# A decoder step on one core: three deferred tiles for four, their loads ahead of the stores of x, and two tags for the PSUM of the down projection

## The chip, the cores and the metric

The kernel runs on one core of a Trainium2 chip. The metric is the device time of one execution in microseconds (us). TensorE does the matrix products, VectorE and ScalarE the elementwise work, GpSimd part of it; all DMAs are issued by SyncE's queue (SPq in the profile). All data are float32; the weight products are made of three products of high and low parts.

## The reference

One inference step of a decoder layer, for a prompt of 1024 tokens and 8 x 8 sample tokens (1088 columns in all, model width 1024):

```python
h = rms_norm(x, norm_mix_g)
proj = h @ w_in
a = silu(layer_norm(depthwise_conv_valid(a_full, ...)))       # convolution heads
o = attend(q, k, v)                                            # dilated attention
x = x + concat([a, o]) @ w_out
h = rms_norm(x, norm_ffn_g)
g_full = concat([ffn_past, h @ w_ffn_gate])
g = depthwise_conv_valid(g_full, ffn_conv_w, ffn_conv_b)
x = x + (silu(g) * (h @ w_ffn_up)) @ w_ffn_down
y = rms_norm(x, norm_final_g)
```

The K and V rows and the last rows of both convolutions are outputs too.

## The kernel before

Everything is held transposed: features on the 128 partitions, tokens along the free dimension. `x` is 8 tiles of 128 features. Weights come in tiles of 128 output features. Every operand of a weight product is split into a high part (ScalarE, a rounding copy) and a low part (a subtraction on VectorE or GpSimd), and `block_product` (L916) and `two_products` (L931) issue three matmuls for each pair of tiles and each chunk of 272 tokens.

The order on each engine and queue is made by a planner from a simulated timeline; the code steers it with `tc.issue_after(i)`, which puts the instructions of a block behind instruction `i` on its engine, and with the number of buffers of each tag. Memory comes in zones; a tile of a new zone waits for the tiles of the old zone whose place it takes.

The stages that matter here:

- **Output projection.** The 8 feature tiles of the mixed heads (`mixed`, spilled to DRAM) go into `w_out` in `PARTS` (3, 3, 2). `out_part` (L855) does a part for all 8 output tiles m, all tokens. In the second part the tiles m in `ORDER[:DEFER]` do only the first half of the tokens (544 columns, `HALF`); the second half of these is deferred.
- **The last part** is done by halves of the tokens: `out_half(0)` and `out_half(1)` (L1099). For each m a pair of PSUM banks (`pair`, L906) takes the product of the last two features, VectorE adds it to x (L1111), x is stored to DRAM (`x2d`, L1112), ScalarE squares it (L1114) and VectorE sums the squares (L1118). In `out_half(1)` the deferred tiles add their three missing features (`deferred`, `wd`). The deferred operands are loaded with L1013 and converted between the tiles of `out_half(0)` (`convert`: `later_input`, L998, `later_weight`, L1004).
- **Second norm.** `root` (L201) sums the squares over the partitions with tiny matmuls and takes the inverse root; `spread` (L226) copies it to all partitions. The first half's root is made inside `out_half(1)` (`norm_first`), the second half's between the first two products of the gate (`between`, `spread_second`).
- **Gated feed-forward, zone F.** The tokens' halves and the weights' halves are combined in seven block products, with their block tiles in the tags b11, b21, b22, t1 to t4 of 8 buffers each. The first pair of weight tiles is done with plain products: `gate0` and `up0` with `first_half` and `second_half`. After it `ffn_pair` for j = 1 to 10 runs the seven products (`products`, L1212), whose PSUM pairs px, py, pz turn in four buffers.
- **Down projection, zone D.** Nine units (14 products) over two groups of features; in each unit four chains m = 0 to 3, each in a PSUM pair, are added to x (L1515). Its first five moving tiles (`ux`) are split by L1409 and L1410, and the last four writers of u in zone F (`late[-4:]`) are put behind the fifth of them on VectorE. `last_product` follows with the last features and the final norm; its PSUM banks come from a pool that is opened where the pairs were.

Of the kernel before, what the change touches and what calls it, by code (L numbers as in the profile page):

```python
# [18 lines left out]
F32 = mybir.dt.float32  # L19
# [5 lines left out]
P = 128  # L25
D = 1024
# [36 lines left out]
ORDER, DEFER = (4, 5, 6, 7, 0, 1, 2, 3), 4  # L63
# [19 lines left out]
def trunk_kernel(tc, xT, w_in, w_out, w_gate, w_up, w_down, par, kc, vc, sa, sf, pmask, smask,  # L83
                 yT, kT, vT, ca, cas, cf):
    nc = tc.nc
    with (
# [112 lines left out]
        rooted, summed = [None], [None]  # L199
# [26 lines left out]
        def spread(r, new, width):  # L226

            size = sizes(width)
            rb = new("rb")
            for c0 in range(0, width, 512):  # L230
                pb = bank(*rbank[0])
                w = min(512, width - c0)
                for i in range(c0 // P, -(-(c0 + w) // P)):
                    n = size[i]
                    summed[0] = nc.tensor.transpose(pb[:, i * P - c0:i * P - c0 + n],
                                                    r[:n, i:i + 1].to_broadcast([n, P]), ident[:n, :n]).ins
                nc.scalar.activation(rb[:, c0:c0 + w], pb[:, :w], AF.Copy)
            return rb
# [667 lines left out]
        def pair(s="g"):  # L906

            return zone[pairs[0] + "ps"].tile([P, 1024], F32, tag="g2", name=nm(s), bufs=pairs[1])
# [59 lines left out]
        n = PARTS[-1]  # L968
        part = []
        for h, tag in enumerate(("b11", "t2")):  # L970
            part.append([])
            for i in range(n):
                raw = slot("b11", "mx", F32)
                last_load = nc.sync.dma_start(raw, mixed[k0 + i][:, h * HN:h * HN + HN]).ins
                hi, lo = early[tag].pop() if early[tag] else slot(tag, "mh"), slot(tag, "ml")
                nc.scalar.activation(hi, raw, AF.Copy)
                nc.vector.tensor_sub(lo, raw, hi.bitcast(F32))
                part[h].append((hi, lo))
# [15 lines left out]
        n1 = PARTS[-2]  # L994
        kd = k0 - n1
        deferred, wd, later = [], {}, []

        def later_input(raw):  # L998
            hi, lo = slot("t3", "mh"), slot("t3", "ml")
            nc.scalar.activation(hi, raw, AF.Copy)  # L1000
            nc.gpsimd.tensor_sub(lo, raw, hi.bitcast(F32))
            deferred.append((hi, lo))

        def later_weight(m, raw):  # L1004
            hi, lo = [slot("b22", t, w=n1 * P) for t in ("wh", "wl")]
            nc.scalar.activation(hi, raw, AF.Copy)
            nc.gpsimd.tensor_sub(lo, raw, hi.bitcast(F32))
            wd[m] = [t.rearrange("p (k c) -> p k c", c=P) for t in (hi, lo)]

        def load_later(dst, src):  # L1010
            nonlocal last_load
            with tc.issue_after(last_load):
                last_load = nc.sync.dma_start(dst, src).ins  # L1013

        for i in range(n1):
            raw = slot("t2", "mx", F32)
            load_later(raw, mixed[kd + i][:, HN:])
            later.append((later_input, raw))
        for m0 in ORDER[:DEFER:2]:
            raw = wp.tile([P, D], F32, tag="WR", name=nm("wr"), bufs=WR)[:, :2 * n1 * P]  # L1020
            load_later(raw.rearrange("p (m c) -> p m c", m=2),
                       w_out[m0:m0 + 2, :, kd * P:k0 * P].rearrange("m p c -> p m c"))
            for i in range(2):
                later.append((later_weight, m0 + i, raw[:, i * n1 * P:(i + 1) * n1 * P]))

        def convert(j, square):
            for call, *args in later[j - 1:j] if j else ():
                with tc.issue_after(square):
                    call(*args)

        blocks = {tag: [None] * 4 for tag in BTAGS}
        made = []

        def split(x, tag, k):
            hi, lo = slot(tag, tag + "h"), slot(tag, tag + "l")
            nc.scalar.activation(hi, x, AF.Copy)
            made.append(nc.vector.tensor_sub(lo, x, hi.bitcast(F32)).ins)
            blocks[tag][k] = hi, lo
# [14 lines left out]
        def weight_parts(x, new, eng):  # L1053
            n = x.shape[-1]
            hi, lo = new
            nc.scalar.activation(hi, x, AF.Copy)
            eng.tensor_sub(lo, x, hi.bitcast(F32))
            hi, lo = [t.rearrange("p (k c) -> p k c", c=P) for t in (hi, lo)]
            return [(hi[:, i:i + 4], lo[:, i:i + 4]) for i in range(0, n // P, 4)]

        def block_tile(x, zone=False, eng=nc.gpsimd):

            if zone:
                t = early["gate"].pop(0) if early["gate"] else zt("F", "WA", 2, "wa", D, F32R)
# [3 lines left out]
            nc.scalar.activation(hi, x, AF.Copy)  # L1068
            eng.tensor_sub(lo, x, hi.bitcast(F32))  # L1069
            return [t.rearrange("p (k c) -> p k c", c=P) for t in (hi, lo)]  # L1070

        def plain_blocks(raw):
            return [block_tile(r[:, i * half:i * half + half], r is raw[0]) for r in raw for i in range(2)]
# [22 lines left out]

        x2d = [dp.tile([P, N], F32, name=f"x2d{m}") for m in range(KT)]

        def out_half(h, hook):  # L1099
# [4 lines left out]
            for j, m in enumerate(ORDER):  # L1104
# [7 lines left out]
                nc.sync.dma_start(x2d[m][:, c], x)  # L1112
                s = slot("t1", "sq", F32)
                square = nc.scalar.activation(s, x, AF.Square).ins  # L1114
# [4 lines left out]
                hook(j, square)  # L1119
# [9 lines left out]
        sq0, _ = out_half(0, convert)  # L1129
        rs = []  # L1130

        def norm_first(j, square):
# [12 lines left out]
        raw, up0 = weight_raw(w_up, 0), []  # L1145
# [25 lines left out]
        def between():  # L1171
            rs.append(root(sq1, D, HN))
            with tc.issue_after(rooted[0]):
                for i in range(2):
# [9 lines left out]
        first_blocks(0, "b11")  # L1184
        first_blocks(4, "b21")
# [171 lines left out]
        pairs[:] = ["D", 4]  # L1357
# [129 lines left out]
        for k, (g, unit) in enumerate(UNITS):  # L1487
# [203 lines left out]
```

## Time and profile before

| | us |
|---|---|
| median of 3 runs | 1345.58 (1344.97 to 1346.34) |
| the profiled execution | 1341.79 |
| its span, first to last instruction | 1340.1 |
| TensorE busy | 1294.4 (97%) |
| VectorE busy | 936.2 (70%) |
| ScalarE busy | 561.6 (42%) |
| GpSimd busy | 486.6 (36%) |

In the profile PE is TensorE, PEld its weight loads, DVE VectorE, ACT ScalarE, POOL GpSimd and SPq SyncE's queue of DMAs. A row names the line of the kernel, the operation and its tiles (out<-in, buffer numbers left out). Times in the views count from the start of the span. Neighbouring matmuls overlap: each lasts some 0.29 us, and a new one starts every 0.125 us.

### The profile page before, as it was taken

To read this page: it belongs to the slowest core of one execution; us is meant where nothing else is said; L and a number is where in the kernel's file an instruction comes from. 1 tells how busy PE (TensorE), PEld (TensorE's weight loads), DVE (VectorE), ACT (ScalarE), POOL (GpSimd) and SP (SyncE) were. 2 spreads that over 40 slices of the span, in tenths; PEclk is the share of its full clock that TensorE was granted. 3 is DMA by queue.
4 is the path that set the end of the run, shared out by engine and by line. 5 is a ranking of instruction groups with operands and counts; after the bars stand their busy time and mean duration, and the time that the engine had idled before them with its cause. 6 is when DMAs were issued, how large, how long until landed. Compare 5 with 4: busy or idle time off the path is not lost.

```text
span 1340.1 us, 25967 instructions
## 1 busy us (share of the span) xinstructions
PE 1294.4 (97%) x10311; PEld 1251.1 (93%) x10311; DVE 936.2 (70%) x1785; ACT 561.6 (42%) x1130; POOL 486.6 (36%) x394
## 2 busy tenths in 40 slices
PE   8999999999989998999999999999999989999996
PEld 7999988998979787999999999999999989999996
DVE  6379879555675666578976767667776549967656
ACT  6412121547575466355443323333333434334432
POOL 1321112111101103640765646555465525445610
PEclk9999999999999999999999999999999999999998
DMA  8248777565789868561033322233222394352412
GB/s 312 58 137 298 277 240 199 174 173 137 219 252 258 259 221 256 166 211 61 11 112 122 110 103 72 83 122 106 106 71 84 123 360 164 107 186 86 156 40 95
DMA packets 93738, 211.90 MB, mean 158 GB/s; under 512 B 13873, under 2 KB 43313, under 8 KB 93617
## 3 DMA queue, kind: packets, MB, share of 16 engines
q1 hardware_dynamic: 93616, 210.24, 48.1%
q8 instruction: 81, 1.33, 0.4%
q14 instruction: 41, 0.33, 0.1%
HBM read 154.17 MB, written 56.04 MB: 157 GB/s over the span
## 4 chain that ended last, share of the span: by engine, by line
PE 81%; DVE 9%; DMA 5%; ACT 2%; issue 1%; POOL 1%; SPq 1%; DVEq 0%; POOLq 0%; ACTq 0%
PE g L186 6%; PE g L187 6%; PE g L188 6%; PE py L928 5%; PE py L927 5%; PE py L925 4%; PE g L925 4%; PE g L928 4%; PE g L927 4%; PE px L925 3%; PE pz L925 3%; PE pz L927 3%; PE pz L928 3%; PE px L928 3%; PE px L927 3%; PE s L657 3%
## 5 line engine op out<-in xcount | busy, mean ns | idle before, releaser
L162 POOL TENSOR_TENSOR wl<-wr,wh 128x1024 fp32r<-128x1024 f32 (+1 forms) x36 | 67.9, 1887 | 271.7 <-PE g L188 166.2
L186 PE MATMUL g<-xh,wh 128*128 128x384 f32 (+1 forms) x472 | 156.9, 332 | 1.5 <-DVE qkv L449 1.4
L187 PE MATMUL g<-xl,wh 128*128 128x384 f32 (+1 forms) x472 | 155.2, 329 | 0.0
L188 PE MATMUL g<-xh,wl 128*128 128x384 f32 (+1 forms) x472 | 155.2, 329 | 0.0
L925 PE MATMUL g<-ux,as 128*128 128x272 f32 x504 | 145.8, 289 | 3.8 <-DVE u L1314 3.4
L928 PE MATMUL g<-ux,as 128*128 128x272 f32 x504 | 146.0, 290 | 0.0
L927 PE MATMUL g<-ux,as 128*128 128x272 f32 x504 | 145.4, 289 | 0.0
L1069 POOL TENSOR_TENSOR wb<-wr,wb 128x512 fp32r<-128x512 f32 x82 | 120.1, 1475 | 55.4 <-ACT wb L1068 55.4
L1425 POOL TENSOR_TENSOR as<-ar,as 128x640 fp32r<-128x640 f32 (+1 forms) x56 | 91.1, 1638 | 107.6 <-ACT as L1424 105.7
L1068 ACT ACTIVATE wb<-wr 128x512 fp32r<-128x512 f32 x84 | 52.5, 627 | 155.7 <-DVE wr L1085 95.1
L1069 POOL TENSOR_TENSOR wa<-wr,wa 128x512 fp32r<-128x512 f32 x42 | 65.4, 1560 | 126.6 <-ACT wa L1068 124.6
L925 PEld LDWEIGHTS g<-ux,as 128*128 128x128 f32 x504 | 95.7, 190 | 4.4 <-issue 4.4
L928 PEld LDWEIGHTS g<-ux,as 128*128 128x128 f32 x504 | 95.5, 190 | 0.0
L927 PEld LDWEIGHTS g<-ux,as 128*128 128x128 f32 x504 | 95.4, 189 | 0.0
L186 PEld LDWEIGHTS g<-xh,wh 128*128 128x128 f32 x472 | 88.7, 188 | 3.9 <-DVE qkv L449 2.2
L1295 DVE SCALAR_TENSOR_TENSOR fc<-gb,prm,fc 128x1104 f32<-128x1104 f32 x44 | 81.5, 1870 | 14.8 <-ACT fc L1293 14.4
L698 ACT ACTIVATE y<-y,m 128x128 f32<-128x128 f32 (+1 forms) x192 | 88.5, 465 | 4.9 <-DVE m L686 4.7
L187 PEld LDWEIGHTS g<-xl,wh 128*128 128x128 f32 x472 | 88.8, 188 | 0.1
L188 PEld LDWEIGHTS g<-xh,wl 128*128 128x128 f32 x472 | 88.8, 188 | 0.1
L160 ACT ACTIVATE wh<-wr 128x1024 fp32r<-128x1024 f32 (+1 forms) x36 | 29.5, 821 | 131.1 <-PE g L188 111.0
L399 DVE SCALAR_TENSOR_TENSOR cacc<-gp,prm,cacc 128x1024 f32<-128x1024 f32 x60 | 84.3, 1405 | 0.1
L661 DVE CUSTOM_DVE_ANT_0 y<-s,pmk 128x128 f32<-128x128 f32 (+1 forms) x192 | 63.6, 377 | 28.9 <-PE s L657 24.2
(379 smaller groups left out, 4297.6 us busy)
## 6 DMA issues: line engine op xcount, KB each, us to landing
cr<-in_kc SPq DMA_DIRECT2D x24, 768.0 KB, 8.0
cr<-in_vc SPq DMA_DIRECT2D x24, 768.0 KB, 7.2
ux<-ub SPq DMA_DIRECT2D x63, 272.0 KB, 4.1
kk<-dk SPq DMA_DIRECT2D x48, 256.0 KB, 5.9
wr<-in_w_gate SPq DMA_DIRECT2D x22, 512.0 KB, 3.3
wr<-in_w_up SPq DMA_DIRECT2D x22, 512.0 KB, 4.4
wr<-in_w_in SPq DMA_DIRECT2D x20, 512.0 KB, 4.7
ub<-u SPq DMA_DIRECT2D x18, 544.0 KB, 4.6
```

What stands on the lines that cost most here:

```text
L162: lo_eng.tensor_sub(lo, raw, hi.bitcast(F32))
L186: nc.tensor.matmul(ps[c], whi[:, k, :], xh[:, t0:t0 + n], start=(k == 0), stop=False)
L187: nc.tensor.matmul(ps[c], whi[:, k, :], xl[:, t0:t0 + n], start=False, stop=False)
L188: nc.tensor.matmul(ps[c], wlo[:, k, :], xh[:, t0:t0 + n], start=False, stop=(k == nk - 1))
L399: eng.scalar_tensor_tensor(acc[:, :S], gp[:, j:j + S], col(w0 + j), acc[:, :S], op0=ALU.mult, op1=ALU.add)
L698: nc.scalar.activation(y, y, AF.Exp, bias=m[:, 4 * g + i:4 * g + i + 1], scale=-1.0, accum_out=den[:, g, 2 * hd + u, i:i + 1])
L925: nc.tensor.matmul(ps, whi[:, k, :], xh[:, t], start=(start and k == 0), stop=False, skip_group_check=True)
L927: nc.tensor.matmul(ps, whi[:, k, :], xl[:, t], start=False, stop=False, skip_group_check=True)
L928: nc.tensor.matmul(ps, wlo[:, k, :], xh[:, t], start=False, stop=(stop and k == nk - 1), skip_group_check=True)
L1069: eng.tensor_sub(lo, x, hi.bitcast(F32))
L1295: nc.vector.scalar_tensor_tensor(c[:, :W], gb[i][:, t:t + W], col(C_FW + 3 * f + t), c[:, :W], op0=ALU.mult, op1=ALU.add)
L1425: nc.gpsimd.tensor_sub(lo, raw, hi.bitcast(F32))
```

## The change

- `DEFER` goes from 4 to 3: tile m=7 does all its tokens in the second part.
- The deferred features are loaded straight into the buffers of their low parts (tag t3), the deferred weights into buffers of their own (tag b22), all right behind the loads of the last part; the conversions follow its high parts on ScalarE and go on without the tiles of `out_half(0)` (`parts_of`).
- The stores of x are put behind these loads on the queue.
- The raw tiles of `w_up`'s first pair get four buffers of tag t2 (halves), no longer the two shared ones of `WR`; those and the `w_gate` tiles are loaded behind the last deferred load.
- The four conversions of `gate0` are put behind the copy of the first root on ScalarE, the four of `up0` behind the fourth `b11` part. The low parts of `up0` are made by GpSimd and not by VectorE.
- The first root is made after the first tile of `out_half(1)` and spread after the second (before: second and third); the first scalings follow the second residual, not the third.
- In zone D the four PSUM pairs of one tag become two tags of two: m = 0, 1 use g3, m = 2, 3 use g2. One unused pair of g2 is taken first, so that g2's place comes first.

```diff
-ORDER, DEFER = (4, 5, 6, 7, 0, 1, 2, 3), 4
+ORDER, DEFER = (4, 5, 6, 7, 0, 1, 2, 3), 3
...
-                nc.scalar.activation(rb[:, c0:c0 + w], pb[:, :w], AF.Copy)
+                copied[0] = nc.scalar.activation(rb[:, c0:c0 + w], pb[:, :w], AF.Copy).ins
...
+        def parts_of(raw, hi, lo):
+            done = nc.scalar.activation(hi, raw, AF.Copy).ins
+            nc.gpsimd.tensor_sub(lo, raw, hi.bitcast(F32))
+            return done
...
+        for i in range(n1):
             hi, lo = slot("t3", "mh"), slot("t3", "ml")
+            raw = lo.bitcast(F32)
+            with tc.issue_after(last_load):
+                last_load = nc.sync.dma_start(raw, mixed[kd + i][:, HN:]).ins
+            with tc.issue_after(last_high):
+                last_high = parts_of(raw, hi, lo)
             deferred.append((hi, lo))
+        for m in ORDER[:DEFER]:
+            raw = slot("b22", "wr", F32, n1 * P)
+            with tc.issue_after(last_load):
+                last_load = nc.sync.dma_start(raw, w_out[m, :, kd * P:k0 * P]).ins
             hi, lo = [slot("b22", t, w=n1 * P) for t in ("wh", "wl")]
+            with tc.issue_after(last_high):
+                last_high = parts_of(raw, hi, lo)
...
-        for i in range(n1):
-            raw = slot("t2", "mx", F32)
-            load_later(raw, mixed[kd + i][:, HN:])
-            later.append((later_input, raw))
-        for m0 in ORDER[:DEFER:2]:
-            raw = wp.tile([P, D], F32, tag="WR", name=nm("wr"), bufs=WR)[:, :2 * n1 * P]
-            load_later(raw.rearrange("p (m c) -> p m c", m=2), ...)
...
+        raw = [r for t in weight_raw(w_gate, 0) for r in split_halves(t)]
+        gate_parts, gate0 = plain_blocks(raw, [*map(split_halves, early["gate"]), new_blocks(), new_blocks()])
+        raw = [slot("t2", "wr", F32, half) for _ in range(4)]
+        for i, r in enumerate(raw):
+            with tc.issue_after(last_load):
+                nc.sync.dma_start(r, w_up[i // 2 * HF][:, i % 2 * half:i % 2 * half + half])
+        tiles = [[t[:, :half] for t in early["up"][i:i + 2]] for i in (0, 2)]
+        up_parts, up0 = plain_blocks(raw, [*tiles, new_blocks(), new_blocks()])
...
-                nc.sync.dma_start(x2d[m][:, c], x)
+                with tc.issue_after(last_load):
+                    nc.sync.dma_start(x2d[m][:, c], x)
...
-        sq0, _ = out_half(0, convert)
+        sq0, _ = out_half(0, lambda j: None)
...
-            if j == 1:
+            if j == 0:
                 rs.append(root(sq0, D, HN))
-            elif j == 2:
+            elif j == 1:
                 rs[0] = spread(rs[0], new_root, HN)
+                order = copied[0]
+                for x in gate_parts:
+                    with tc.issue_after(order):
+                        order = parts_of(*x)
...
-                with tc.issue_after(made[-2] if len(made) > 1 else residuals[2]):
+                with tc.issue_after(made[-2] if len(made) > 1 else residuals[1]):
...
-        gate0 = plain_blocks(weight_raw(w_gate, 0))
-        raw, up0 = weight_raw(w_up, 0), []
...
         def between():
             rs.append(root(sq1, D, HN))
-            with tc.issue_after(rooted[0]):
-                for i in range(2):
-                    up0.extend(weight_parts(raw[0][:, i * half:i * half + half], early["up"][2 * i:2 * i + 2],
-                                            nc.vector))
-                up0.extend(block_tile(raw[1][:, i * half:i * half + half], eng=nc.vector) for i in range(2))
...
         first_blocks(0, "b11")
+        order = high[0]
+        for x in up_parts:
+            with tc.issue_after(order):
+                order = parts_of(*x)
         first_blocks(4, "b21")
...
-        pairs[:] = ["D", 4]
+        pairs[:] = ["D", 2]
+        pair()
...
-                        chain[m] = pair()
+                        chain[m] = pair("g", "g3" if m < 2 else "g2")
```

More of the change, by code (lines that the diff above doesn't have):

```diff
@@ L1026, in convert @@
[L1026 to L1029, printed above, removed]
         blocks = {tag: [None] * 4 for tag in BTAGS}
[L1032 removed]
+        made, high = [], [None]
         def split(x, tag, k):
             hi, lo = slot(tag, tag + "h"), slot(tag, tag + "l")
[L1036 removed]
+            high[0] = nc.scalar.activation(hi, x, AF.Copy).ins
             made.append(nc.vector.tensor_sub(lo, x, hi.bitcast(F32)).ins)
@@ L1051, in weight_raw, with block_tile @@
             return raw
[L1053 to L1061, printed above, removed]
+        def block_tile(x, zone=False):
             if zone:
-                t = early["gate"].pop(0) if early["gate"] else zt("F", "WA", 2, "wa", D, F32R)
+                t = zt("F", "WA", 2, "wa", D, F32R)
             else:
```

45 lines of the change are left out of this document (18 added, 27 removed).

## The prediction

> **What bounds the kernel now.** I read the page's busy times first, then the busy time by stretches of 5 us (columns: length, busy time and instruction count of TensorE, its weight loads, VectorE, ScalarE and GpSimd, then the granted TensorE clock).
>
> ```profile
> PE 1294.4 (97%) x10311; PEld 1251.1 (93%) x10311; DVE 936.2 (70%) x1785; ACT 561.6 (42%) x1130; POOL 486.6 (36%) x394
> ```
>
> TensorE is busy 97% of the span, so a change can gain only where TensorE waits, or where it runs at a lower clock. Three such places lie in code that the change touches.
>
> ```profile
> 560.00:565.00 5.00, 2.81 (x14) 2.37 (x14) 3.00 (x3) 3.75 (x6) 4.41 (x4) 0.80 0.71 254
> 565.00:570.00 5.00, 5.00 (x37) 5.00 (x36) 2.52 (x4) 0.69 (x2) 0.00 (x0) 0.86 0.16 59
> 570.00:575.00 5.00, 5.00 (x42) 5.00 (x41) 4.85 (x8) 4.14 (x7) 2.37 (x2) 1.00 0.88 205
> 575.00:580.00 5.00, 2.84 (x18) 2.18 (x18) 4.63 (x6) 3.25 (x7) 5.00 (x4) 1.00 1.04 394
> 580.00:585.00 5.00, 5.00 (x30) 5.00 (x29) 1.54 (x2) 0.16 (x1) 3.47 (x3) 0.66 0.75 242
> ...
> 600.00:605.00 5.00, 5.00 (x42) 5.00 (x41) 5.00 (x8) 2.64 (x4) 0.00 (x0) 1.00 0.39 142
> ...
> 615.00:620.00 5.00, 3.54 (x31) 3.26 (x30) 2.14 (x9) 2.04 (x5) 0.00 (x0) 1.00 0.00 0
> ```
>
> ```profile
> 1075.00:1080.00 5.00, 5.00 (x42) 5.00 (x42) 2.67 (x6) 1.97 (x3) 0.22 (x1) 1.00 0.93 325
> 1080.00:1085.00 5.00, 1.60 (x14) 1.42 (x13) 4.97 (x8) 0.00 (x0) 0.00 (x0) 1.00 1.02 358
> 1085.00:1090.00 5.00, 5.00 (x30) 5.00 (x29) 1.50 (x4) 1.95 (x3) 0.00 (x0) 0.66 1.03 404
> ```
>
> An undisturbed stretch holds 42 matmuls of 272 columns. So 560 to 570 misses 33 of 84, which is 33 / 42 x 5 = 3.9 us (a); 575 to 585 misses 36, 4.3 us (b); 615 to 620 misses 11, 1.3 us (c); 1080 to 1090 misses 40, 4.8 us (d). The list of waits from 560 to 1082 (us in total, times, longest) says for whom TensorE waited, and its own timeline where (start, length, and in brackets the idle time before).
>
> ```profile
> PE py L928 <- POOL wb L1069: 1.8, 1, 1.8
> PE g L925 <- ACT mh L976: 1.7, 1, 1.7
> PE g L235 <- DVE rr L223: 1.5, 1, 1.5
> PE g L925 <- ACT wh L1006: 1.3, 2, 0.9
> PE g L928 <- POOL wl L1007: 0.9, 1, 0.9
> ```
>
> ```profile
> 560.08 0.28 PE L188 MATMUL g<-mh,wl 128*128 128x272 f32 x1
> 562.07 0.77 PE L925 MATMUL g<-mh,wh 128*128 128x272 f32 x4 [1.71 <-ACT mh L976]
> ...
> 1084.41 0.36 PE L925 MATMUL g<-ux,as 128*128 128x272 f32 x1 [3.40 <-DVE u L1314]
> ```
>
> (a) is the start of the last output part (L976), (b) the deferred weights (L1006, L1007), (c) the second root (L223), (d) the first down projection, which waits for an eviction. After 1.7, 2.2 and 3.4 us of waiting a slow stretch follows (clock 0.80 and 0.86, 0.66, 0.66); after 1.5 us in (c) the clock stays 1.00. [...]
>
> **The change part by part.** *Three tiles deferred.* For m=7 the second half (3 features x 3 products x 2 chunks, 18 matmuls) moves from the last output half to the part before it: 18 / 42 x 5 = 2.1 us. No work is saved, but TensorE now ends that part at 560.36 + 2.1 = 562.5, after ScalarE's first high part let it go on at 562.07. Loads and conversions that (a) waited for do not depend on m=7's extra products. Left in (a): the first pair of PSUM banks may wait for m=7's last eviction, 0.72 us by the eviction rows below. Bounds 0 and the whole 3.9; I take 0.7, because 1.5 us in (c) cost no clock. Gain 3.2.
>
> *Loads ahead of the stores.* The DMA queue's timeline:
>
> ```profile
> 558.53 1.33 SPq L974 DMA_DIRECT2D mx<-mixed  x3
> 568.23 0.32 SPq L1112 DMA_DIRECT2D x2d<-x  x1
> 568.65 1.67 SPq L1013 DMA_DIRECT2D mx<-mixed  x3
> 570.42 0.90 SPq L1013 DMA_DIRECT2D wr<-in_w_out  x2
> ```
>
> and GpSimd's:
>
> ```profile
> 572.63 5.54 POOL L1001 TENSOR_TENSOR ml<-mx,mh 128x544 fp32r<-128x544 f32 x3 [8.22 <-ACT mh L1000]
> 578.13 5.34 POOL L1007 TENSOR_TENSOR wl<-wr,wh 128x384 fp32r<-128x384 f32 x4
> 587.08 2.52 POOL L1069 TENSOR_TENSOR wa<-wr,wa 128x512 fp32r<-128x512 f32 x2 [3.61 <-ACT wa L1068]
> 589.57 3.00 POOL L1069 TENSOR_TENSOR wb<-wr,wb 128x512 fp32r<-128x512 f32 x2
> 638.03 9.58 POOL L1069 TENSOR_TENSOR wa<-wr,wa 128x512 fp32r<-128x512 f32 x1 [45.46 <-ACT wa L1068]
> ```
>
> The deferred loads left at 568.65 to 571.3, behind the first store. Now they follow the loads that end at 559.9, so some 8.8 us earlier; the conversions that began at 572.63 can begin near 564 to 566. Three feature lows and one weight low take 5.54 + 5.34 / 4 = 6.9 us, done near 572.5. TensorE needs them after the first half's 96 matmuls (11.4 us) at 562.5 + 0.7 + 11.4 = 574.6. So (b) goes, 4.3; at worst 1.5 of it stays (no landing time was kept). The queue gets three issues more (three weight tiles for two pairs, four halves of `w_up` for two tiles), 1.33 / 3 = 0.44 us each; with the twelve loads it is through by about 565.2, before the first store of x has anything to store at 568.23: nothing lost, and if it were, the scaling that rewrites x would wait for the store.
>
> *Weights bound later, root a tile earlier.* The four `w_gate` conversions follow the copy of the first root, the four of `w_up` follow the fourth `b11` high part and go from VectorE to GpSimd. The gate's 2.52 + 3.00 = 5.5 us of GpSimd have a tile of 30 matmuls and five of 12 to hide behind, 90 matmuls or 10.7 us; beyond that the first gate product would wait. The root's products move from the second tile to the first, 30 matmuls or 3.6 us. VectorE is full behind it (5.00 of 5.00 at 600). What GpSimd costs it:
>
> ```profile
> 577.86 3.78 DVE L1118 TENSOR_TENSOR sq<-sq,sq 128x544 f32<-128x544 f32 x3 [0.26 <-ACT sq L1114]
> ...
> 645.73 0.72 DVE L1206 TENSOR_TENSOR x<-x 128x544 f32<-128x544 f32 x1
> 646.37 0.65 DVE L1278 TENSOR_TENSOR gb<-pv,ta 128x480 f32<-128x480 f32 x1
> ...
> 1079.23 3.26 DVE L1410 TENSOR_TENSOR ux<-ux 128x544 fp32r<-128x544 f32 x5 [0.21 <-DMA x<-x2d]
> 1082.41 1.22 DVE L1305 TENSOR_TENSOR u<-u,fc 128x480 f32<-128x480 f32 x2
> 1083.55 0.72 DVE L1314 TENSOR_TENSOR u<-pz,u 128x544 f32<-128x544 f32 x1
> ```
>
> Beside GpSimd an addition took 1.26 instead of 0.72, so eight conversions put 8 x 0.54 = 4.3 us on VectorE there. The root comes 3.6 earlier, but TensorE arrives 2.1 earlier in this stage for the moved work: 4.3 + 2.1 - 3.6 = 2.8 us less in hand before the `b21` parts are needed. If the slack covers that it costs 0, if there was none 2.8; I take the middle, 1.4. Four subtractions of about 0.72 leave VectorE behind the second root, which only offsets the wait for that root's copy: nothing. With `w_up` ready early, TensorE has its products to run while the second root is worked out, so (c) can go; the order is the planner's, so I take half, 0.65. The wait of 1.8 for `wb` (L1069) stays: it hangs on VectorE's chain, which comes forward about as much as TensorE.
>
> *Two PSUM tags.* TensorE ends the stage at 1084.41 - 3.40 = 1081.0 and waits until the eviction at 1083.55 has ended. That eviction stands behind five low parts (1079.23) and two products. With m=0 and m=1 in other banks the first chain needs only the low parts, the fifth at 1082.5, which TensorE would reach 13 matmuls (1.5 us) after 1081.0: just in time. So (d) goes, 4.8. Price: the banks of m=2 and m=3 now come first in the tail's order, and its first product may wait for m=3's eviction: 0 to 0.72, I take 0.4. Within the stage each chain keeps its own bank: nothing.
>
> Sum: 3.2 + 4.3 + 0.65 + 4.8 - 1.4 - 0.4 = 11.15. The profiled execution took 1341.79, 3.8 below the median of the runs, 1345.58; I take the difference from the median: **1334.4**.
>
> **The rivals.**
> 1. *Conversions starve (slower).* The GpSimd subtraction at 638.03 took 9.58 us, and ended 1.24 us after the first VectorE instruction with an operand in PSUM (646.37) had begun. If the four `w_up` conversions meet VectorE full of SBUF work, the third is done 28.7 us after they begin. They begin with the fourth `b11` part, about when the first gate product starts, and TensorE needs the third after two products of 48 matmuls, 11.4. It would wait 17.3, then 3.9 for the fourth (9.6 less 5.7 of product), and two slow stretches of 1.4 (as in d, 4.8 - 3.4) follow: 24.0, against a gain of 11.15: 1358.4. It decides from 6.4 us for each conversion (4 x 6.4 - 11.4 - 5.7 + 2.8 = 11.3). Against it: evictions from PSUM stand among these VectorE instructions, and each lets a conversion in. [...]
> 2. *The bank of m=0 is still the last one freed.* The trace names no bank. (d) stays, the tail's price goes: 1338.8.
> 3. *The slow stretches are not the waits' doing.* Waits go, slowness turns up elsewhere: (a) 3.9 - 1.7 and (b) 4.3 - 2.2 stay, 1338.7. For it: (c) shows that waiting need not cost clock. Against it: the slow rows stand right behind (a), (b) and (d) and nowhere between. [...]
> 4. *The opening gains nothing*: new waits take the place of (a), (b), (c), only (d) counts: 4.8 - 1.4 - 0.4 = 3.0, 1342.6.
> 5. *The change does nothing*: both, 1345.6.
>
> **How the numbers follow.** What a measurement of this kernel can tell is about 0.2%, 2.7 us. Forecast 0.46, its own range 1331 to 1337.5; rival 2 0.12, rival 3 0.09, rival 4 0.12, rival 5 0.09, rival 1 0.12. Rival 4 lies at the bound, so half of it counts as same: faster 0.46 + 0.12 + 0.09 + 0.06 = 0.73, same 0.15, slower 0.12. The range 1331 to 1345 leaves out rival 1, part of 5 and a rest below.
>
> **What would show it.** (a): no wait over 1 us at L925 before the first output half, no slow stretch there. (b): no wait on the deferred lows, their loads ahead of the first store. (c): no wait at L235 in the second spread. (d): the first L925 of the down projection starts before the eviction of `pz`. Rival 1 shows as GpSimd subtractions of several us near the first gate products. The prediction is wrong if TensorE waits longer there, or if the first down projection starts no earlier after the last `pz`.

## The result and the profile after

The changed kernel took 1337.61 us (median of 7 runs, 1334.33 to 1341.21) against 1345.58 (by now 7 runs, 1340.92 to 1352.47): ratio 0.9936, 95% interval 0.9908 to 0.9965. A second series on another chip gave 0.9937 (0.9912 to 0.9962). The forecast was 1334.4, the range 1331 to 1345. So the sign and the range held, and of the forecast gain of 11.15 us the medians show 8.0. The trace shows that the parts of the sum did not come out alike.

The profiled execution took 1335.22, its span is 1333.4, 6.7 less than before. The stretches of 5 us of the changed kernel (columns as in the prediction):

```profile
560.00:565.00 5.00, 3.73 (x27) 3.27 (x25) 2.96 (x4) 2.98 (x5) 2.50 (x3) 1.00 1.00 354
565.00:570.00 5.00, 5.00 (x42) 5.00 (x41) 4.04 (x7) 2.62 (x5) 1.80 (x1) 1.00 0.99 333
...
575.00:580.00 5.00, 3.99 (x30) 3.56 (x28) 4.79 (x6) 2.15 (x4) 2.84 (x3) 1.00 0.55 208
580.00:585.00 5.00, 4.69 (x28) 4.69 (x29) 1.71 (x9) 0.87 (x2) 0.00 (x0) 0.71 0.16 59
...
600.00:605.00 5.00, 4.27 (x32) 4.05 (x32) 5.00 (x6) 4.52 (x9) 4.38 (x3) 1.00 0.29 102
605.00:610.00 5.00, 2.52 (x18) 2.30 (x19) 5.00 (x6) 1.96 (x4) 2.08 (x2) 1.00 0.18 70
```

```profile
1080.00:1085.00 5.00, 5.00 (x40) 4.87 (x40) 4.97 (x8) 3.42 (x6) 1.32 (x1) 1.00 1.04 404
1085.00:1090.00 5.00, 5.00 (x42) 5.00 (x41) 3.38 (x5) 0.99 (x2) 1.99 (x2) 1.00 1.05 397
```

The hole before the down projection (d) is gone: 40 and 42 matmuls. So is the slow stretch behind the opening (560 to 570). But there is a slow stretch at 580 to 585 again (clock 0.71), and 600 to 610, which was full before, now misses 34 of 84 matmuls. The list of TensorE's waits from 560 to 620 names what is new:

```profile
PE px L945 <- DVE b11l L1027: 1.7, 1, 1.7
PE px L943 <- ACT ta L1158: 1.5, 1, 1.5
PE g L208 <- DVE sq L1118: 1.1, 1, 1.1
PE g L925 <- ACT mh L986: 0.7, 1, 0.7
PE g L927 <- DVE ml L987: 0.6, 1, 0.6
...
PE g L928 <- POOL wl L976: 0.2, 1, 0.2
```

The last three are what is left of (a) and (b). The first three did not exist before: the first root waits for the sum of squares (L1118), the first gate products wait for the fourth low part (L1027), and the products behind them for the copy of the gate's PSUM (L1158) that follows.

**Distances inside one execution.** The two profiled executions of the changed kernel differ by 7.2 us, and almost all of that lies ahead of the change. So I count each profile from A, the end of the last matmul of the part before (L188), less the 2.14 us that m=7 adds there where it is no longer deferred (the prediction's 18 / 42 x 5; a row of the stretches also counts the matmuls that only reach into it, and at one start every 0.125 us it is 2.25, so the distances of the kernels that defer three tiles are 0.1 too small beside those that defer four). TensorE's timeline of the changed kernel at these places:

```profile
560.82 0.31 PE L188 MATMUL g<-mh,wl 128*128 128x320 f32 x1
...
580.31 1.18 PE L208 MATMUL g<-ones,sq 128*128 128x1 f32 x10 [1.13 <-DVE sq L1118]
...
598.88 0.29 PE L943 MATMUL px<-b11h,wa 128*128 128x272 f32 x1
...
614.52 1.10 PE L208 MATMUL g<-ones,sq 128*128 128x1 f32 x10
...
617.81 0.39 PE L943 MATMUL px<-b11h,wa 128*128 128x272 f32 x1
...
1078.57 0.28 PE L928 MATMUL pz<-t4h,wb 128*128 128x272 f32 x1
1078.69 0.30 PE L925 MATMUL g<-ux,as 128*128 128x272 f32 x1
```

A is 560.82 + 0.31 - 2.14 = 558.99. The first gate product comes 598.88 - 558.99 = 39.89 later, the first up product 58.82, the end of zone F's last product 519.86. The table has the same distances for every profile. "Hole" is the time from that end to the first matmul of the down projection (they overlap by 0.16 where there is none), "rest" what follows to the end of the span, "A to end" the whole. The ratio is that of the runs to those of the kernel before, with its interval.

| kernel | A to gate | gate to up | A to up | A to zone F's end | hole | rest | A to end | ratio of runs |
|---|---|---|---|---|---|---|---|---|
| before | 43.40 | 15.87 | 59.27 | 520.65 | 3.40 | 255.69 | 779.7 | 1 |
| changed | 39.89 | 18.93 | 58.82 | 519.86 | -0.16 | 254.71 | 774.4 | 0.9936 (0.9908 to 0.9965) |
| changed, again | 39.31 | 18.95 | 58.26 | 519.34 | -0.16 | 254.83 | 774.0 | 0.9937 (0.9912 to 0.9962) |
| tags alone | 42.82 | 15.87 | 58.69 | 520.21 | -0.16 | 254.66 | 774.7 | 0.9969 (0.9952 to 0.9986) |
| changed, one tag | 39.86 | 19.81 | 59.67 | 519.21 | 3.41 | 253.42 | 776.0 | 0.9995 (0.9973 to 1.0017) |
| w_up later | 39.79 | 18.39 | 58.18 | 519.02 | -0.16 | 254.43 | 773.3 | 0.9953 (0.9932 to 0.9974) |
| w_up on VectorE | 39.75 | 15.97 | 55.72 | 517.80 | -0.16 | 253.57 | 771.2 | 0.9934 (0.9912 to 0.9956) |
| w_gate early | 39.79 | 17.61 | 57.40 | 517.27 | -0.16 | 253.52 | 770.6 | 0.9947 (0.9926 to 0.9968) |
| all eight early | 39.90 | 15.68 | 55.58 | 514.70 | -0.16 | 254.14 | 768.7 | 0.9906 (0.9882 to 0.9930) |
| root later | 37.05 | 22.24 | 59.29 | 518.89 | -0.16 | 254.40 | 773.1 | 0.9970 (0.9950 to 0.9989) |
| eight early, root later | 38.79 | 14.45 | 53.24 | 513.09 | -0.16 | 254.41 | 767.3 | 0.9883 (0.9858 to 0.9908) |
| defer three alone | 39.06 | 14.82 | 53.88 | 515.09 | 3.40 | 256.60 | 775.1 | 0.9936 (0.9915 to 0.9956) |
| defer three, tags | 38.67 | 14.44 | 53.11 | 512.87 | -0.16 | 254.69 | 767.4 | 0.9910 (0.9882 to 0.9939) |
| combined | 36.93 | 14.43 | 51.36 | 513.43 | -0.15 | 254.19 | 767.5 | 0.9912 (0.9884 to 0.9941) |

The two profiles of the changed kernel agree within 0.6 us in A to end; the intervals of the runs are 0.3 to 0.6% wide, 4.6 to 7.7 us. So the distances tell the mechanisms apart, and the runs say whether they add up. Below, a distance of the changed kernel is that of its first profile. By distances the change gained 5.3 and 5.7 us: 4.5 and 4.4 in the hole and the rest, only 0.8 and 1.3 in the whole opening.

### The profile page after: what moved, and what is told of

Same layout as the page of the kernel before. It is cut to its first block, busy times and chain, and to the rows that moved or that the text cites. A ratio compares the mean times of both kernels' runs of the same rounds, so it can differ in the third digit from the quotient of the medians.

```text
span 1333.4 us, 25958 instructions
## 1 busy us (share of the span) xinstructions
PE 1289.9 (97%) x10302; PEld 1248.1 (94%) x10302; DVE 933.8 (70%) x1782; ACT 561.8 (42%) x1129; POOL 488.5 (37%) x397
## 4 chain that ended last, share of the span: by engine, by line
PE 81%; DVE 10%; DMA 4%; issue 2%; ACT 1%; SPq 1%; POOL 0%; DVEq 0%; POOLq 0%; ACTq 0%
PE g L186 6%; PE g L187 6%; PE g L188 6%; PE py L928 5%; PE py L925 5%; PE py L927 5%; PE g L925 4%; PE g L927 4%; PE g L928 4%; PE pz L927 3%; PE pz L928 3%; PE pz L925 3%; PE px L925 3%; PE px L928 3%; PE px L927 3%; PE s L657 3%
## 5 line engine op out<-in xcount | busy, mean ns | idle before, releaser
L188 PE MATMUL g<-xh,wl 128*128 128x384 f32 (+1 forms) x472 | 155.2, 329 | 0.0
L1051 POOL TENSOR_TENSOR wb<-wr,wb 128x512 fp32r<-128x512 f32 x80 | 116.2, 1462 | 56.2 <-ACT wb L1050 56.2
L1051 POOL TENSOR_TENSOR wa<-wr,wa 128x512 fp32r<-128x512 f32 x40 | 62.8, 1572 | 105.8 <-ACT wa L1050 105.7
L188 PEld LDWEIGHTS g<-xh,wl 128*128 128x128 f32 x472 | 88.8, 188 | 0.1
```

The source lines that it names most:

```text
L188: nc.tensor.matmul(ps[c], wlo[:, k, :], xh[:, t0:t0 + n], start=False, stop=(k == nk - 1))
L1051: nc.gpsimd.tensor_sub(lo, x, hi.bitcast(F32))
```

## The experiments

**Tags alone.** The kernel before, with nothing but the two tags.

```diff
...
-        pairs[:] = ["D", 4]
+        pairs[:] = ["D", 2]
+        pair()
...
-                        chain[m] = pair()
+                        chain[m] = pair("g", "g3" if m < 2 else "g2")
```

> The kernel before, with the two PSUM tags of the down projection alone. Theory: the first chain no longer needs the pair that the last pz held, so the whole hole of 1080 to 1090 (40 matmuls of 84, 4.8 us) goes: 4.8 us faster than before, 40 matmuls more in that stretch, and the first product starts before the eviction of pz. Rival: the tags pay only together with the earlier stage; then the hole stays at 3 us or more and the time is that of before.

Measured 1339.53 against 1343.5, 4.0 less. The stretches of that kernel:

```profile
1080.00:1085.00 5.00, 5.00 (x42) 5.00 (x42) 2.80 (x6) 1.01 (x2) 0.00 (x0) 1.00 0.90 313
1085.00:1090.00 5.00, 5.00 (x40) 4.87 (x40) 4.29 (x8) 1.00 (x2) 0.00 (x0) 1.00 0.97 334
```

No wait and no slow stretch. The tags carry (d) by themselves.

**Changed, one tag.** The same edit the other way round, in the changed kernel.

> The changed kernel, with the down projection's pairs back in one tag of four. Theory: it keeps only what the opening brings, and that is little, since 1.7 + 1.5 us of new waits at the first gate products and 1.1 at the first root stand against what (a) and (b) gave: 1 to 3 us faster than before, 4 to 5 slower than the changed kernel, and TensorE waits some 3.4 us again before the first down projection. Rival (each term as I forecast it): the opening is worth 3.2 + 4.3 + 0.65 - 1.4 = 6.8 us, and this kernel is about 6.8 faster than before.

Measured 1341.91 against 1343.5, ratio 0.9995: the opening by itself can't be told from nothing. The wait of 3.40 is back. (By distances it is 3.7, of which 2.3 lie in the rest, where the clock happened to stay full; see the rivals below.) The opening as forecast (6.8) is refuted: the interval ends at 0.9973, 3.6 us.

**The w_up conversions later.** Where the gain of the opening went: VectorE's timeline of the changed kernel while GpSimd works on `w_up` (600.62 to 607.1):

```profile
601.15 1.82 DVE L1124 SCALAR_TENSOR_TENSOR x<-x,prm,rb 128x544 f32<-128x544 f32 x1
602.89 1.34 DVE L1110 TENSOR_TENSOR x<-g,x 128x544 f32<-128x544 f32 x2
604.16 1.78 DVE L1027 TENSOR_TENSOR b11l<-x,b11h 128x544 fp32r<-128x544 f32 x1
605.86 1.80 DVE L1124 SCALAR_TENSOR_TENSOR x<-x,prm,rb 128x544 f32<-128x544 f32 x1
```

```profile
588.73 2.63 POOL L976 TENSOR_TENSOR wa<-wr,wa 128x512 fp32r<-128x512 f32 x2 [9.14 <-ACT wa L975]
591.31 3.51 POOL L976 TENSOR_TENSOR wb<-wr,wb 128x512 fp32r<-128x512 f32 x2
600.62 3.51 POOL L976 TENSOR_TENSOR wa<-wr,wa 128x512 fp32r<-128x512 f32 x2 [5.80 <-ACT wa L975]
604.09 2.99 POOL L976 TENSOR_TENSOR wb<-wr,wb 128x512 fp32r<-128x512 f32 x2
```

A scaling or a low part takes 0.71 to 0.78 alone and 1.8 here; the eviction from PSUM (L1110, 1.34 for two) takes no longer than elsewhere. VectorE is busy 5.00 of 5.00 us in both stretches (600 to 610, above), so every stretched instruction delays the parts behind it and with them the second root. The edit:

```diff
         first_blocks(0, "b11")
+        first_blocks(4, "b21")
         order = high[0]
         for x in up_parts:
             with tc.issue_after(order):
                 order = parts_of(*x)
-        first_blocks(4, "b21")
```

> The changed kernel, with the four w_up conversions behind the last b21 high part, not behind the fourth b11 high part. Theory (GpSimd beside a full VectorE is what gave the gain back): VectorE's instructions at 601.15, 604.16 and 605.86 took 1.80 us each beside these conversions and 0.71 to 0.78 alone, so its chain up to the last b21 part ends 3.1 us earlier; TensorE's wait of 1.7 for b11l goes and that of 1.5 for ta shrinks or goes, and the second root is reached 2.5 to 3 us earlier. The conversions then run beside the root and must be done for the first up product: 0 to 1.5 us of that are lost to a wait there. In all 1 to 3 us faster than the changed kernel. Rival (VectorE's amount of work, not the contention, sets the second root): root at the same time, nothing gained, and up to 4 us lost at the first up product.

Measured 1337.06 against 1343.5. The second root's products came 52.32 us after A, for 55.53 in the changed kernel: 3.2 earlier, as the contention predicts. But the first up product came only 0.6 earlier: the conversions now lay beside the root's own chain, and the spread waited 2.0 us. Of this kernel, VectorE:

```profile
615.48 0.17 DVE L221 TENSOR_TENSOR rt<-rr 128x5 f32<-128x5 f32 x1 [0.27 <-ACT rr L218]
615.68 1.19 DVE L222 SCALAR_TENSOR_TENSOR rt<-rt,rv 128x5 f32<-128x5 f32 x1
616.90 1.19 DVE L223 SCALAR_TENSOR_TENSOR rr<-rt,rr 128x5 f32<-128x5 f32 x1
```

An instruction on five columns took 1.19 instead of 0.17. So the cause is confirmed and the remedy is not; by the runs it can't be told from the changed kernel.

**The w_gate conversions early.**

```diff
+        for x in gate_parts:
+            with tc.issue_after(last_high):
+                last_high = parts_of(*x)
...
-                order = copied[0]
-                for x in gate_parts:
-                    with tc.issue_after(order):
-                        order = parts_of(*x)
```

> The changed kernel, with the four w_gate conversions right behind the deferred ones, not behind the copy of the first root. Theory (contention): GpSimd is idle from 579.6 to 588.7 and VectorE nearly so from 580.8 to 587.0; put there, the conversions no longer stretch VectorE's instructions at 590.78, 592.49 and 593.59 (1.15, 1.18 and 1.81 us for 0.71, 0.78 and 0.71: 1.9 us), so the b11 parts come up to 1.9 us earlier and the wait of 1.7 for b11l shrinks by as much. 1 to 2 us faster than the changed kernel. Rivals: the conversions push the end of the first sum of squares (an addition of 1.26 us each beside GpSimd) and the wait before the first root grows past 1.1 us: no gain, or 1 us slower; or the first wait on b11l goes and the wait on the ta evictions grows by the same: no change.

Measured 1336.3 against 1343.5. The first up product came 1.4 us earlier than in the changed kernel (57.40), within the 1 to 2 expected; the wait for `b11l` is gone and that of 1.46 for `ta` stays. The wait before the root did not grow (1.14), but the wait of 1.46 before the second spread, which the change had removed, is back. By the runs it can't be told from the changed kernel.

**The w_up low parts on VectorE**, behind the second root, as before the change.

```diff
             rs.append(root(sq1, D, HN))
+            with tc.issue_after(rooted[0]):
+                for x in up_parts:
+                    parts_of(*x, nc.vector)
...
         first_blocks(0, "b11")
-        order = high[0]
-        for x in up_parts:
-            with tc.issue_after(order):
-                order = parts_of(*x)
```

> The changed kernel, with the low parts of w_up on VectorE behind the second root, as in the kernel before, not on GpSimd behind the fourth b11 part. Theory (contention): as with the w_up conversions late, the second root's products come 3.2 us sooner than in the changed kernel (52.3 us after the end of the part before, changed kernel 55.53), but no conversion is late for the first up product, which only pays the wait of 1.46 us for the spread: at 55.5 to 56 (changed kernel: 58.82). 3 us faster than the changed kernel. Rival: the four subtractions on VectorE (4 x 0.71 us) delay the spread or the b22 parts by as much as they save: no change.

Measured 1336.28 against 1344.27. First up product at 55.72, forecast 55.5 to 56: 3.1 earlier than in the changed kernel. The same stage of VectorE, from this kernel:

```profile
602.09 0.78 DVE L1124 SCALAR_TENSOR_TENSOR x<-x,prm,rb 128x544 f32<-128x544 f32 x1
602.78 1.35 DVE L1110 TENSOR_TENSOR x<-g,x 128x544 f32<-128x544 f32 x2
604.05 0.71 DVE L1027 TENSOR_TENSOR b11l<-x,b11h 128x544 fp32r<-128x544 f32 x1
```

Where these conversions are done, on GpSimd beside the scalings or on VectorE behind the root, makes 3.1 us before the first up product (engine and place were changed together). Part of it is given back behind it: at zone F's end 1.5 to 2.1 are left (517.80 for 519.34 and 519.86). The four subtractions stand on VectorE ahead of the second root's scalings, as the rival says: these begin 2.19 us after the spread's first matmul, in the changed kernel 1.38 (in all six profiles with the subtractions there 2.19, in the others 1.38 to 1.84). In the next pair TensorE then waits 1.84 for `wb` (L1051), in the changed kernel 1.00.

**All eight early.** Both groups right behind the deferred conversions (the edit as for w_gate, for `up_parts` too).

> The changed kernel, with all eight w_gate and w_up conversions right behind the deferred ones. Theory: GpSimd works them off between 580 and 592, mostly while VectorE waits for the first root; none is left beside VectorE's chain of scalings and parts. In the two runs before, the time from the end of the part before (less 2.14 us for m=7) to the second root's products was 55.53 us in the changed kernel, 54.11 with the gate's conversions early and 52.32 with the w_up ones late; here 51 to 52. The w_up parts are ready, so no wait comes for them: 3 to 5 us faster than the changed kernel. Rival (the second root only moves a wait: VectorE's parts come earlier, but the spread of the second root then has TensorE wait 1.46 us, as in the kernel before, and the end of the pair stays where it is): root earlier by 3.5, pair's end earlier by 2 at most, time of the changed kernel within 2 us.

Measured 1333.66 against 1346.08, the changed kernel on the same chip 1337.13. Second root at 52.30, first up product at 55.58 and zone F's end 4.6 to 5.2 earlier than in the changed kernel; the spread's wait of 1.46 did come, as the rival said. The slow stretch behind the first root stayed. Of the 4.6 to 5.2, 1.4 is a slow stretch in zone F that this profile did not have (see the rivals below).

**Root later**, in the changed kernel:

```diff
-            if j == 0:
+            if j == 1:
                 rs.append(root(sq0, D, HN))
-            elif j == 1:
+            elif j == 2:
...
-                with tc.issue_after(made[-2] if len(made) > 1 else residuals[1]):
+                with tc.issue_after(made[-2] if len(made) > 1 else residuals[2]):
```

> The changed kernel, with the first root made after the second tile and spread after the third, as in the kernel before; conversions where the change has them. Theory (a tile earlier, TensorE stands in order behind the root's products, whose last sum is not there): the wait of 1.13 us at the root and the slow stretch behind it go, as they did with the eight conversions early, where the first up product came 2.3 us sooner for it (55.58 to 53.24 us after the end of the part before, less 2.14 for m=7). Here VectorE's chain beside GpSimd sets the second root, so part of it is lost again: first up product at 56.5 to 58.8 (the changed kernel: 58.82), 0 to 2.3 us faster than the changed kernel, no stretch of under 36 matmuls at 580 to 590. Rival (the earlier root was worth its tile): first up product at 60 or later, slower by 1 us or more.

Measured 1338.9 against 1344.27. The first gate product came 2.84 us earlier than in the changed kernel (37.05 for 39.89): wait and slow stretch are gone. The first up product came no earlier (59.29, forecast 56.5 to 58.8, the rival 60 or later), because VectorE, now later and as slow beside GpSimd, has TensorE wait 1.5, 1.5 (for `ta`) and 1.7:

```profile
PE px L945 <- DVE b21l L1027: 1.7, 1, 1.7
PE px L945 <- DVE b11l L1027: 1.5, 2, 1.3
```

**Eight early, root later.** Both edits.

> As the run with all eight conversions early, with the first root made after the second tile and spread after the third, as in the kernel before. Theory (the slow stretch at 580 to 585 hangs on the wait of 1.13 us for the first half's last sum): the wait and the slow stretch go together (1.13 + 14 missing matmuls x 0.119 = 1.7 us), the spread comes 3.6 - 2.8 = 0.8 us later, and TensorE has the b21 parts in time: 1 to 2.8 us faster than the other. Rival (the slow stretch is not the wait's doing): 30 or fewer matmuls in one of the stretches behind the root all the same, and the time is the other's within 1 us.

Measured 1330.53 against 1346.08: ratio 0.9883, the interval ends at 0.9908 where that of the changed kernel on the same chip begins at 0.9912. This version beats both kernels. First up product 2.34 us earlier than with the early root. The slow stretch is gone, though TensorE then waits 1.64 for the first spread, whose root the conversions stretch (1.25, 1.22 and 1.18 for L221 to L223).

**Defer three alone.** The kernel before, with m=7 no longer deferred.

```diff
-ORDER, DEFER = (4, 5, 6, 7, 0, 1, 2, 3), 4
+ORDER, DEFER = (4, 5, 6, 7, 0, 1, 2, 3), 3
...
-            for i in range(2):
+            for i in range(2 if m0 + 1 in ORDER[:DEFER] else 1):
                 later.append((later_weight, ...))
```

> The kernel before, with three deferred tiles for four and nothing else: m=7 is done in the part before, its loads and conversions leave. Theory (the moved 18 matmuls only cover the start of the last part): the waits for the first high and low parts shrink from 1.71 + 0.48 to 0.6 + 0.6 as in the changed kernel, and no slow stretch follows: the opening 2.5 to 3.2 us shorter, and VectorE's chain still is not hit by more GpSimd work than before. The deferred parts' waits (0.85, 0.44, 0.86) stay or grow, since TensorE reaches them sooner by 2.1 + 1 us less for m=7 and they are converted as before: so 0 to 2 us faster in all. Rival (as forecast, (a) by itself is a gain of 3.2): 3 us faster.

Measured 1338.5 against 1346.08, ratio 0.9936: by the runs as much as the whole change (5.9 to 11.4 us by the interval), by the distances only 4.6, with the hole still there. The two do not meet, and what lies ahead of A in the runs is not known. I had expected 0 to 2, the rival 3. The waits and the stretches of this kernel from 565:

```profile
PE g L925 <- ACT wh L1006: 1.0, 2, 0.6
PE g L927 <- DVE ml L977: 0.8, 1, 0.8
PE g L925 <- DVE x L870: 0.7, 1, 0.7
```

```profile
580.00:585.00 5.00, 3.97 (x28) 3.37 (x28) 4.90 (x6) 3.00 (x6) 4.89 (x5) 1.00 1.05 403
585.00:590.00 5.00, 5.00 (x42) 5.00 (x41) 2.57 (x3) 1.50 (x3) 1.49 (x2) 1.00 0.93 282
```

The opening's waits are 1.5 (changed kernel: 1.3). The deferred parts, loaded and converted as before, are late by 1.0 and not 2.2, with no slow stretch behind them. Nothing else is added: GpSimd has no more to do beside VectorE than before, and the first up product stands at 53.88, 4.9 earlier than in the changed kernel.

**Defer three and tags.**

> The kernel before, with only DEFER 3 and the two PSUM tags: no early loads, no later bound weights, root where it was. Theory (these two are all that the change gains, the rest gives some back): first up product at 53.9 us as with DEFER 3 alone (before: 59.27), the hole of 1080 to 1090 gone: 5.4 + 4.8 = 10.2 us faster than before, 2 us faster than the changed kernel. Rival (the loads ahead of the stores carry part of the gain): not faster than the changed kernel.

Measured 1332.76 against 1344.27, ratio 0.9910. First up product at 53.11, the hole gone, A to end 12.3 shorter than before. The two plain pieces give 7 us more by the distances than the change that contains them (1.4 of it is the slow stretch in zone F, which this profile did not have); by the runs the interval (0.9882 to 0.9939) still overlaps that of the changed kernel.

**Combined.** w_gate early, w_up on VectorE behind the second root, first root later.

> The changed kernel, with three steps put elsewhere: w_gate's conversions right behind the deferred ones, w_up's low parts on VectorE behind the second root, the first root a tile later. Theory: with all eight early, the four of w_up at 587 to 592 stretched the root's own small VectorE instructions (1.25, 1.22 and 1.18 us for 0.17) and cost a wait of 1.64 us at the first spread; here that wait goes, and no GpSimd work lies beside the scalings: first up product at 52 to 53.2, 14 to 17 us faster than before, at most 1.6 faster than the kernel with all eight early and the root later. Rival: the wait only moves to the second spread (1.46), and the time is that kernel's within 1 us.

Measured 1332.97 against 1344.27, ratio 0.9912, below the forecast 14 to 17. Up to the first up product it did what was forecast (51.36, even 0.6 under the range), and there TensorE waits for nothing but the opening (0.7, 0.6 and 0.2).

But zone F's end comes no earlier (513.43 for 513.09 with eight early and root later). The 1.9 us that it is ahead last until the next pair. There TensorE waits 1.81 for `wb` and not 1.02, as with w_up on VectorE, and then runs 14 matmuls slowly, some 1.4 us, where the other kernel ran none.

**The changed kernel again**, as the measure beside these:

> The changed kernel as it is, beside the next ones on one chip: about 8 us faster than before, as measured at first.

1337.13 against 1346.08.

## Why the prediction came out as it did

**(d), two tags: right.** Forecast 4.8 less 0.4. Measured 3.56 (hole) + 0.98 (rest) = 4.54. The first product started at 1078.69, and the eviction that it had waited for ran later:

```profile
1081.39 0.72 DVE L1315 TENSOR_TENSOR u<-pz,u 128x544 f32<-128x544 f32 x1
```

Tags alone give the same. The rest varies by over 1 us among kernels with the same tail, so only the hole is known well; the price of 0.4 in the tail can't be seen.

**(a), the start of the last part: right, short by 0.6.** Forecast 0.7 left. The wait of 0.68 stands (in several of these kernels it is put down to L870, the last eviction, as forecast). A second one of 0.60 for the low part was not in the sum. The clock stayed 1.00.

**(b), the deferred weights: the wait went, the gain did not.** The loads went ahead of the stores and 0.19 us of waiting was left. But the deferred conversions did not begin "near 564 to 566", 1.5 to 3.5 us after the end of the part before (562.5). The first high part stands on ScalarE behind the first tile's square:

```profile
566.72 0.66 ACT L1114 ACTIVATE sq<-x 128x544 f32<-128x544 f32 x1 [3.42 <-DVE x L1110]
567.28 0.64 ACT L975 ACTIVATE mh<-ml 128x544 fp32r<-128x544 f32 x1
```

GpSimd began at 568.00, 6.9 after that end (561.13), and the first weight's low part was done 14.2 after it, forecast 10.0. It was almost in time by luck: TensorE, forecast there after 12.1, came after 14.1. So GpSimd was still at work until 579.58, beside the last sums of squares. And the step "the root's products move from the second tile to the first" was booked as 3.6 us in hand. I never asked whether its input would be there. The products stand in TensorE's order behind the first tile, and the sum of squares came 1.13 later, on a VectorE stretched by the deferred conversions:

```profile
576.49 3.68 DVE L1118 TENSOR_TENSOR sq<-sq,sq 128x544 f32<-128x544 f32 x3
```

1.23 us for an addition of 0.71. The 30 matmuls behind the root took 581.42 to 586.96, 5.5 us instead of 3.8. So 1.13 + 1.7 + 0.19 of the 4.3 were lost again; root later shows the 1.13 and the 1.7 gone. The loads ahead of the stores were worth little to begin with: with DEFER 3 alone only 1.0 of waiting is left without them.

**(c), the second root's wait: gone for another reason.** TensorE now runs the last ten matmuls of `b21` behind the root's, so the spread finds its root ready. That also happens with DEFER 3 alone, where `w_up` is converted as before, and with w_gate early or all eight early, where no matmul stands between, the wait of 1.46 is back. So it is the order, not the early weights.

**The contention: the term that failed.** Its size was right. Eight conversions stretched VectorE by 0.43 + 0.40 + 1.09 + 1.04 + 1.06 + 1.02 = 5.0 us (590 to 608), for a forecast of 4.3. But I let only 1.4 count, for a slack that the 3.6 of the root was to fill, and the sum left out what else lies on VectorE's chain. From the first scaling to the last low part of `b21` it is, in the kernel before,

```profile
594.59 1.48 DVE L1124 SCALAR_TENSOR_TENSOR x<-x,prm,rb 128x544 f32<-128x544 f32 x2 [0.49 <-ACT rb L237]
...
611.51 0.72 DVE L1037 TENSOR_TENSOR b21l<-x,b21h 128x544 fp32r<-128x544 f32 x1
```

and in the changed kernel

```profile
588.16 0.79 DVE L1124 SCALAR_TENSOR_TENSOR x<-x,prm,rb 128x544 f32<-128x544 f32 x1 [0.43 <-ACT rb L237]
590.78 1.15 DVE L1118 TENSOR_TENSOR sq<-sq,sq 128x544 f32<-128x544 f32 x1 [1.84 <-ACT sq L1114]
...
613.42 0.71 DVE L1027 TENSOR_TENSOR b21l<-x,b21h 128x544 fp32r<-128x544 f32 x1
```

17.6 and 26.0 us, 8.3 longer: 5.0 of stretching, a wait of 1.84 for a square that stands on ScalarE behind the four `w_gate` conversions (588.01 to 590.1), and the rest three more additions (L1110, L1118), which now lie behind the earlier root. Against A the chain starts 34.23 and 29.17 us on, so 5.1 earlier, and ends 51.9 and 55.1 on, so 3.3 later, while TensorE comes to the gate 3.5 earlier. From first gate to first up product it took 18.93, before 15.87: 3.1 lost. With both groups of conversions out of the way and a later root it is 14.45.

**The sum.** By distances the opening gave 0.8 to 1.3 instead of 6.75 (3.2 + 4.3 + 0.65 - 1.4), which is the fourth rival (only (d) counts), not the forecast. The signs that the prediction named all came, but for 0.19 at (b): none of them looked at the waits that took the place of the old ones. And the range held partly by its width, for the fourth rival's 1342.6 lies in it too. That the median stands 8.0 below and not 5.5 lies within the interval (0.9908 is 12.4, 0.9965 is 4.7), and what the part ahead of A adds to it is open.

**The other rivals.** Conversions did not starve: 1.3 to 1.8 us each (rows above). The one that was slow before, of the next pair, is slow still (8.80 for 9.58). The bank of m=0 was not the last one freed. That slow stretches are not the waits' doing alone has support: after the same wait of 3.40 us at the same place, three kernels (in order: the kernel before, whose row stands in the prediction, then defer three alone, then changed with one tag) went on at 0.66, at 0.51, and at 1.00:

```profile
1085.00:1090.00 5.00, 5.00 (x25) 5.00 (x24) 1.89 (x3) 1.74 (x3) 0.00 (x0) 0.51 1.03 401
```

```profile
1085.00:1090.00 5.00, 1.60 (x14) 1.42 (x13) 4.97 (x9) 0.84 (x2) 0.00 (x0) 1.00 1.04 404
1090.00:1095.00 5.00, 5.00 (x42) 5.00 (x42) 2.22 (x4) 1.62 (x3) 0.32 (x1) 1.00 1.05 398
```

That last one explains 1.4 of the 2.3 us by which the rest of that kernel is shorter than before. So the length of a wait did not settle what followed it. Behind the first root, in all seven profiles with the early root, a wait of 1.13 to 1.15 with 1.2 us of ten one-column matmuls is followed by a slow stretch (lowest clock of 5 us: 0.66 to 0.82); in the three with the later root the same ten matmuls come without a wait, and no slow stretch follows (1.00). Whether the wait would do it without the ten matmuls was not tried.

**A slow stretch that the prediction overlooked.** It says that the slow rows stand behind (a), (b) and (d) and nowhere between. There is a fourth in zone F, where TensorE waits 0.5 and then 1.75 for `wb`, in the kernel before:

```profile
660.00:665.00 5.00, 3.25 (x14) 3.02 (x15) 5.00 (x7) 2.98 (x5) 5.00 (x3) 0.69 0.00 0
```

In the changed kernel the second wait is 1.0, not "1.8 stays", and the slow stretch follows all the same (clock 0.66). Here too the same wait can go either way. Right behind 1.81 and 1.77 us the combined kernel and then defer three with tags went on like this:

```profile
665.00:670.00 5.00, 5.00 (x36) 5.00 (x35) 4.99 (x5) 0.00 (x0) 5.00 (x7) 0.82 0.28 68
```

```profile
665.00:670.00 5.00, 5.00 (x42) 5.00 (x42) 5.00 (x5) 0.63 (x1) 5.00 (x7) 1.00 0.20 43
```

Seven of the fourteen profiles have this stretch (12 to 15 matmuls that start 0.23 us apart instead of 0.125, some 1.4 us): before, both of the changed kernel, tags alone, w_up on VectorE, defer three alone, combined. So two distances to zone F's end can differ by 1.4 us without an edit doing it.

## What to carry to other kernels

When a step is moved forward, put two times beside each other: when the engine reaches it, and when its input is ready; here a root a tile earlier stood in TensorE's order ahead of work that could have run. Before giving GpSimd elementwise work with SBUF operands, look at what VectorE does in those microseconds: the same eight conversions, put where VectorE mostly waits, made A to the end 5.3 to 5.7 us shorter, some 4 without the slow stretch in zone F. And when a change has several pieces, run the smallest alone: DEFER 3 and the two tags, seven lines, came to 0.9910.

## What the runs showed of the hardware

- In these runs a VectorE instruction with two SBUF operands took up to 1.1 us longer where it met one on GpSimd, long and short ones alike: up to 1.8 us for 0.71 to 0.78 with 544 columns (changed kernel), 1.19 for 0.17 with five (w_up later), beside GpSimd instructions of 1.25 to 1.8 us. An addition with one operand in PSUM (L1110) took no longer there: 1.34 for two in the changed kernel, 1.35 with w_up on VectorE, where no GpSimd conversion ran beside them.
- The other way round it was not one instruction for one: the GpSimd conversion of the next pair took 8.80 us in the changed kernel, in a stretch where VectorE ran twelve instructions of 0.73 us from SBUF alone, and 9.62 with everything combined. The conversion behind it in the changed kernel took 1.29.
- The part of the program ahead of the change spread A from 558.99 to 568.53 us over fourteen profiles. Distances from a fixed instruction repeated to 0.6 us in the one kernel profiled twice.
